# Two-layer diffusion backbone on one core: where the convolution filters and the Fourier part are computed

## Chip, cores and metric

One core of a Trainium2 chip runs the whole program in one launch. The metric is the device time of one execution in microseconds, median over runs. In the profile PE is TensorE, PEld its weight loads, DVE VectorE, ACT ScalarE, POOL GpSimd, SP SyncE.

## The reference

384 tokens (128 context, 256 latent) of width 1024 pass through two layers. A layer is a half-step feed-forward (SwiGLU, inner width 2816), a token mixer and another half-step feed-forward, each behind an RMS norm scaled and shifted by a modulation made from `c` (latent) or `c_ctx` (context). The mixer's heads are three groups: a Hyena convolution over 256 channels, neighbourhood attention (6 heads) and windowed grouped-query attention (6 query heads, 2 key heads). The convolution's filter depends on weights alone, not on x:

```python
hid  = sin(freq[0] * (feats @ w1 + b1))            # feats: L x 33
hid  = sin(freq[1] * (hid @ w2 + b2))              # L x 64
taps = (hid @ w3).reshape(L, 2, 256) * exp(-t * deltas)
kf   = rfft(concat(taps[:, 0], 0, taps[:0:-1, 1]))
x0, x1, v = split(short_conv(u)); z = x1 * v
y    = x0 * (irfft(rfft(z, 2L) * kf)[:L] + z * skip)   # context (L=128), latent (L=256)
```

## The kernel before

Activations lie with channels on partitions, 384 tokens in the free dimension; weights are float32, each split into a high and a low part, and `mm3` (L303) makes a product of three matmuls (L305 to L307). The weights' order is fixed in `jobs`; `issue`, `ahead` and `get` (L164 to L192) load them ahead through SP's queue, which brings all loads in the order in which they are written, into four buffers, and split them on ScalarE (L142) and VectorE (L143). Each engine executes its instructions in the order in which the Python code writes them.

**Start.** `start(j)` (L1133) prepares the eight chunks of the first feed-forward half; between two chunks' `up` products (18 matmuls each, 144 in all) it is called again, with `mid=True` inside them. The modulation of this half comes in three column chunks for scale and shift, q = 0 and 1: `chunk_load` (L262) loads them, `chunk_rows` (L272) multiplies them with `ct` on TensorE in groups of 32 columns (tile `adm`), `chunk_cols` (L283) turns rows to columns. `square_chunk` (L323), `stats1` and `stats2` make the reciprocal root of the mean square (`rsqrt`, L309; here on VectorE, elsewhere on GpSimd). Later modulation is made on VectorE (L206).

**Mixer.** `mixer(l)` (L536) writes seven projections (`project`, L708: four blocks of 2 k, or two of 4); after each block they call `work(budget)`. `bg` holds generators; `work` advances each one step, from the first on, as long as its budget, which each step's yielded cost lowers, is above nothing; `BUD` holds 1.55 and 3.3 for projections, 1.3 for attention.

```python
BUD = (1.55, 3.3, 1.3)
conv_it = add(conv_bg()); filt_it = add(filt())
drain(q_it); drain(k_it); drain(conv_it); drain(filt_it)
fft_it = add(fft())
```

`conv_bg` (L695) makes u and the short convolution, `filt` (L583) this layer's filter: two sine layers (`sin_layer`, L518), taps in three groups, spectrum (`tf`, 13 matmuls of 256 columns) into the tables K1, K2, K3. `na_post`, `gk_post` and `gq_post` norm and turn queries and keys. `drain` runs a generator to its end. Then `slot` (L972) is called 15 times: slot s writes the scores of unit s (12 units: six head pairs, two query blocks), the norm of unit s-1, the turn of the probabilities of s-2 (`un_turn`, L927: transposes into `pp`, copies into `PT`, which has two buffers), the values of s-3 when that pair is full (`un_pv`, L941), the exponentials, and `work(BUD[2])`. `fft` (L781) runs in these slots: turns of z, three transforms (`zf`) with six products on VectorE each (L809 to L814), two inverse transforms (`cv`, L821). Blocks of the output projection (`wout_block`, L1074) stand between the last slots; the one that needs the convolution's output comes behind `drain(fft_it)`.

Of the kernel before, what the change touches and what calls it, by code (L numbers as in the profile page):

```python
# [7 lines left out]
F32 = mybir.dt.float32  # L8
# [6 lines left out]
P = 128  # L15
# [32 lines left out]
HD = 64  # L48
# [11 lines left out]
for _name, _w in (  # L60
    ("ada_b", DEPTH * NADA * KD), ("norm_g", DEPTH * 3 * KD), ("conv_w", DEPTH * 3 * 6), ("conv_b", DEPTH * 6),
    ("skip", DEPTH * 2), ("naq", DEPTH), ("nak", DEPTH), ("fb1", DEPTH), ("fb2", DEPTH), ("freq", DEPTH * 2),
    ("fscale", 3), ("sel", 2),
):
    SM[_name] = (_n, _w)
    _n += _w
# [13 lines left out]
def _build(ctx, tc, nc, A):  # L80
# [6 lines left out]
    ptp = ctx.enter_context(tc.tile_pool(name="ptp", bufs=2))  # L87
# [29 lines left out]
    load(A["ct"], ct)  # L117
    for k in range(KD):
        load(A["xT"][:, k], xT[k])
    sml = cst.tile([P, NSM], F32, name="sml")  # L120
    load(A["sml"], sml)
    ident = cst.tile([P, P], F32, name="ident")
    load(A["ident"], ident)
# [13 lines left out]
    fw1 = cst.tile([33, DEPTH, HD], F32, name="fw1")  # L137
    fw2 = cst.tile([HD, DEPTH, HD], F32, name="fw2")
# [104 lines left out]
    S.activation(ct[:, :, 0:2], ct[:, :, 0:2], AF.Silu)  # L243
# [266 lines left out]
    fbm = []  # L510
    for l in range(DEPTH):
        fbm.append([cst.tile([P, 1], F32, name=f"fbm{l}{i}") for i in range(2)])

    def sin_bias(l):
        for i, nm in enumerate(("fb1", "fb2")):
            V.tensor_tensor(fbm[l][i], small(nm, l), small("freq", l * 2 + i), op=ALU.mult)

    def sin_layer(pin, fb, fr, out):  # L518
        arg = tt("arg", w=NT)[:HD]
        S.activation(arg, pin, AF.Identity, scale=fr[:HD], bias=fb[:HD])  # L520
        yield 0.1
        kq = tt("kq", w=NT)[:HD]
# [8 lines left out]
        yield 2.3  # L531
        S.activation(out, arg, AF.Sin)
        yield 0.1


    def mixer(l, after):  # L536
# [20 lines left out]
        def loads():  # L557
# [25 lines left out]
        def filt():  # L583
            Cc, Sc = (X["dft"][0][:, i * P:(i + 1) * P] for i in range(2))
            Cl, Sl = X["dft"][1:3], X["dft"][3:5]
# [789 lines left out]
```

## Time and profile before

| | us |
|---|---|
| median of three runs | 1543.93 |
| the runs | 1543.81, 1543.93, 1544.58 |
| the profiled execution | 1544.34 |
| its span, first to last instruction | 1542.6 |
| TensorE, VectorE, ScalarE, GpSimd busy | 1505.7, 1139.4, 672.6, 70.7 |

The busy times are sums over the span; where in it an engine waits, and for whom, has to be read from the timeline of that stretch. A matmul's time in it includes a tail that the next one overlaps, so that the distance from start to start is the better measure; x2 and the like are that many instructions in one row.

### The profile page before, as it was taken

The page shows a single profiled execution, that of the slowest core. Times are in us where ns is not written, and L with a number is a line of the kernel's source. Part 1 is how long each engine was busy: PE and PEld are TensorE (multiplying, and loading weights), DVE is VectorE, ACT ScalarE, POOL GpSimd, SP SyncE. Part 2 cuts the span into 40 slices and gives each one's busy share as a digit, 9 for nine tenths or more (in the row PEclk, how much of TensorE's full clock was granted, in tenths as well). Part 3 has the DMA queues.
Part 4 walks back from the last instruction along what each step waited for, and adds up shares of the span by engine and source line. Part 5 has one row for each costly group of instructions (what it writes and reads, how often), then busy time and mean ns, then how long its engine had stood idle before and what let it go on. Part 6 is the DMA issues. An engine that isn't in the chain of part 4 may idle for free. (4 is left out here: it accounts for less than half of the span.)

```text
span 1542.6 us, 23084 instructions
## 1 busy us (share of the span) xinstructions
PE 1505.7 (98%) x8652; PEld 1444.0 (94%) x8652; DVE 1139.4 (74%) x2158; ACT 672.6 (44%) x1234; POOL 70.7 (5%) x181
## 2 busy tenths in 40 slices
PE   6999999999989999999999999999999999999999
PEld 3999999999768999999999999999996699999998
DVE  4489888879787788877758898787897767544344
ACT  4533333446566454333434433343556655433221
POOL 0000000013300000000000000000141000000000
PEclk9999999999999999999999999999999999999999
DMA  9656665664403446555544565566543034343442
GB/s 307 236 184 237 219 223 201 218 195 149 129 30 117 153 148 220 207 212 187 187 162 139 188 244 209 207 221 202 172 124 109 26 111 138 134 149 108 149 152 72
DMA packets 89733, 261.27 MB, mean 169 GB/s; under 512 B 10097, under 2 KB 27796, under 8 KB 89492
## 3 DMA queue, kind: packets, MB, share of 16 engines
q1 hardware_dynamic: 89236, 258.74, 49.1%
q8 instruction: 68, 1.11, 0.3%
q0 software_dynamic: 384, 1.05, 0.2%
q14 instruction: 45, 0.37, 0.1%
HBM read 257.13 MB, written 2.62 MB: 168 GB/s over the span
## 5 line engine op out<-in xcount | busy, mean ns | idle before, releaser
L143 DVE TENSOR_TENSOR wlo<-raw,whi 128x1024 fp32r<-128x1024 f32 (+2 forms) x352 | 394.4, 1126 | 122.6 <-ACT whi L142 122.5
L305 PE MATMUL up<-mh,whi 128*128 128x384 f32 (+1 forms) x1408 | 479.3, 340 | 4.9 <-ACT mh L142 4.9
L306 PE MATMUL up<-ml,whi 128*128 128x384 f32 (+1 forms) x1408 | 477.4, 339 | 0.7 <-DVE ml L143 0.4
L307 PE MATMUL up<-mh,wlo 128*128 128x384 f32 (+1 forms) x1408 | 477.3, 339 | 0.8 <-DVE wlo L143 0.6
L142 ACT ACTIVATE whi<-raw 128x1024 fp32r<-128x1024 f32 (+2 forms) x352 | 338.4, 974 | 264.4 <-PE dn L306 128.2
L206 DVE CUSTOM_DVE_ANT_0 junk<-adaw,cb,sml 128x1024 bf16<-128x1024 f32 x256 | 332.7, 1300 | 1.9
L305 PEld LDWEIGHTS up<-mh,whi 128*128 128x128 f32 x1408 | 265.8, 189 | 8.7 <-ACT mh L142 6.3
L306 PEld LDWEIGHTS up<-ml,whi 128*128 128x128 f32 x1408 | 265.6, 189 | 2.5 <-DVE ml L143 2.1
L307 PEld LDWEIGHTS up<-mh,wlo 128*128 128x128 f32 x1408 | 266.0, 189 | 2.1 <-DVE wlo L143 2.1
L305 PE MATMUL dn<-gh,whi 128*128 128x384 f32 x704 | 237.4, 337 | 0.0
L306 PE MATMUL dn<-gl,whi 128*128 128x384 f32 x704 | 237.2, 337 | 0.0
L307 PE MATMUL dn<-gh,wlo 128*128 128x384 f32 x704 | 237.1, 337 | 0.0
L142 ACT ACTIVATE gh<-t 128x384 fp32r<-128x384 f32 x76 | 39.9, 525 | 273.0 <-DVE t L485 263.3
L307 PEld LDWEIGHTS dn<-gh,wlo 128*128 128x128 f32 x704 | 132.2, 188 | 0.0
L305 PEld LDWEIGHTS dn<-gh,whi 128*128 128x128 f32 x704 | 132.2, 188 | 0.0
L306 PEld LDWEIGHTS dn<-gl,whi 128*128 128x128 f32 x704 | 132.2, 188 | 0.0
L305 PE MATMUL pj<-whi,mh 128*128 128x384 f32 (+1 forms) x240 | 80.1, 334 | 1.0 <-DVE hyt L362 1.0
L485 DVE TENSOR_TENSOR t<-up,t 128x384 f32<-128x384 f32 x72 | 40.0, 556 | 55.0 <-PE up L307 54.8
L307 PE MATMUL pj<-whi,ml 128*128 128x384 f32 (+1 forms) x240 | 78.3, 326 | 0.0
L306 PE MATMUL pj<-wlo,mh 128*128 128x384 f32 (+1 forms) x240 | 78.2, 326 | 0.0
L143 DVE TENSOR_TENSOR gl<-t,gh 128x384 fp32r<-128x384 f32 x76 | 42.5, 559 | 45.0 <-ACT gh L142 45.0
L326 ACT ACTIVATE sq<-xT 128x384 f32<-128x384 f32 x42 | 22.0, 525 | 100.6 <-DVE xT L385 99.3
(222 smaller groups left out, 1582.9 us busy)
## 6 DMA issues: line engine op xcount, KB each, us to landing
raw<-w SPq DMA_DIRECT2D x184, 512.0 KB, 4.4
adaw<-ada SPq DMA_DIRECT2D x128, 512.0 KB, 3.5
raw<-w SPq DMA_DIRECT2D x64, 448.0 KB, 4.3
raw<-win SPq DMA_DIRECT2D x48, 384.0 KB, 4.0
raw<-w13a SPq DMA_DIRECT2D x32, 384.0 KB, 4.0
adw<-ada SPq DMA_DIRECT2D x32, 192.0 KB, 4.3
raw<-woa SPq DMA_DIRECT2D x16, 384.0 KB, 3.2
nab<-nab SPq DMA_DIRECT2D x24, 192.0 KB, 2.5
```

Source lines behind the costliest of these rows:

```text
L142: S.activation(hi, src, AF.Copy)
L143: V.tensor_tensor(lo, src, hi.bitcast(F32), op=ALU.subtract)
L206: V.tensor_tensor_reduce(out=junk, in0=w, in1=cb[:, v, :], scale=scale, scalar=small("ada_b", (l * NADA + p) * KD + j), op0=ALU.mult, op1= ...
L305: T.matmul(out, ah, bh, start=start, stop=False)
L306: T.matmul(out, ah, bl, start=False, stop=False)
L307: T.matmul(out, al, bh, start=False, stop=stop)
L326: S.activation(sq, xT[j], AF.Square)
L485: V.tensor_tensor(t1, PQ[1][:, :NT], t1, op=ALU.mult)
```

## The change

The new class `Filters` makes the filters of both layers in `start(0)`: the layers lie side by side (on 64 partitions each in the sine layers, on 256 columns each in the spectrum, so that a spectrum matmul has 512 columns), and the spectrum stays in `kft[0]` (in the buffer that later holds `PT`) and `kft[1]`. Both matrices of the third filter layer are loaded and their sum and difference `wsd` taken ahead of the product; the taps of token 0, which have one side only, are made by extra one-row operations. Its loads, sine layers, taps and spectrum are written ahead of the first `up` product, between the parts that were there. `filt`, its loads in the mixer and K3 are gone; `fft` mends row 0 for the first two transforms instead. `chunk_rows` takes scale and shift in one PSUM tile, `chunk_cols` both at once; the reciprocal root of the start goes to GpSimd (`stats1()`). `conv_bg` and `fft` are one generator, `hyena`, drained ahead of attention; in a slot the values of s-3 are written ahead of the turn of s-2, and `PT` has one buffer. The diff, without the host's tables and a few renamed tiles:

```diff
-    ptp = ctx.enter_context(tc.tile_pool(name="ptp", bufs=2))
+    ptp = ctx.enter_context(tc.tile_pool(name="ptp", bufs=1))
...
     def chunk_load(c):
         a, b = CHUNK[c]
         n = (b - a) * P
-        for q in range(2):
-            firsts[c, q] = [tt("adw", w=NT) for _ in range(KD)]
-            for k, t in enumerate(firsts[c, q]):
-                load(A["ada0"][q, k, :, a * P:b * P], t[:, :n])
+        firsts[c] = [[tt("adw", w=NT) for _ in range(2)] for _ in range(KD)]
+        for k in range(KD):
+            for q in range(2):
+                load(A["ada0"][q, k, :, a * P:b * P], firsts[c][k][q][:, :n])
 
     adm = {}
 
-    def chunk_rows(c, q):
+    def chunk_rows(c):
         a, b = CHUNK[c]
         n = (b - a) * P
-        pm = ps("adm", "ab"[q])
-        for k, t in enumerate(firsts.pop((c, q))):
-            o = 32 * (k % 4)
-            T.matmul(pm[o:o + 32, :n], ct[:, k], t[:, :n], start=(k < 4), stop=(k >= 4))
+        pm = ps("adm", "a")
+        for k, w in enumerate(firsts.pop(c)):
+            for q in range(2):
+                o = 64 * q + 32 * (k % 2)
+                T.matmul(pm[o:o + 32, :n], ct[:, k], w[q][:, :n], start=(k < 2), stop=(k >= KD - 2))
         rows = tt("adr", w=NT)
         S.activation(rows[:, :n], pm[:, :n], AF.Copy)
-        adm[c, q] = pm, rows
-
-    def chunk_cols(c, q):
+        adm[c] = pm, rows
+
+    def chunk_cols(c):
         a, b = CHUNK[c]
         n = b - a
-        pm, rows = adm.pop((c, q))
-        o = pm[:, NT:NT + 2 * n]
+        pm, rows = adm.pop(c)
+        o = pm[:, NT:NT + 4 * n]
         for i in range(n):
-            T.matmul(o[:, 2 * i:2 * i + 2], rows[:, i * P:(i + 1) * P], small("sel", 0, 2), start=True, stop=True)
-        o = o.rearrange("p (j v) -> p j v", v=2)
+            T.matmul(o[:, 4 * i:4 * i + 4], rows[:, i * P:(i + 1) * P], small("sel", 0, 4), start=True, stop=True)
+        o = o.rearrange("p (j q v) -> p j q v", q=2, v=2)
 
         def wide(t):
             return t.rearrange("p (j o) -> p j o", o=1).to_broadcast([P, n, 2])
 
-        if q:
-            V.tensor_tensor(mod[0][:, 0, a:b], o, wide(small("ada_b", a, n)), op=ALU.add)
-        else:
-            t = gsc[0][:, 0, a:b]
-            V.tensor_tensor(t, o, wide(small("norm_g", a, n)), op=ALU.mult)
-            V.tensor_tensor(t, t, wide(gb0[:, a:b]), op=ALU.add)
-        done.update((0, 1 - q, j) for j in range(a, b))
+        t = gsc[0][:, 0, a:b]
+        V.tensor_tensor(t, o[:, :, 0], wide(small("norm_g", a, n)), op=ALU.mult)
+        V.tensor_tensor(t, t, wide(gb0[:, a:b]), op=ALU.add)
+        V.tensor_tensor(mod[0][:, 0, a:b], o[:, :, 1], wide(small("ada_b", a, n)), op=ALU.add)
+        done.update((0, p, j) for p in range(2) for j in range(a, b))
 
...
-    def sin_layer(pin, fb, fr, out):
-        arg = tt("arg", w=NT)[:HD]
-        S.activation(arg, pin, AF.Identity, scale=fr[:HD], bias=fb[:HD])
-        yield 0.1
-        kq = tt("kq", w=NT)[:HD]
+    def sin_layer(pin, i, out):
+        fb = sm("fbm", 1)
+        V.tensor_tensor(fb, small("fb", i), small("freq", i), op=ALU.mult)
+        arg = tt("arg", w=NT)
+        S.activation(arg, pin, AF.Identity, scale=small("freq", i), bias=fb)
+        kq = tt("kq", w=NT)
...
+    class Filters:
+        def load_a(self):
+            self.fw1 = load(A["fw1"], tt("fw1", w=P)[:33])
+            self.feats = load(A["feats"], tt("feats", w=NT)[:33])
+            load(A["sml"], sml)
+            self.fw2 = load(A["fw2"], tt("fw2", w=HD))
+
+        def load_b(self):
+            self.w3 = [load(A["fw3"][:, i * HY:(i + 1) * HY], tt("w3", w=HY)) for i in range(2)]
+
+        def load_c(self):
+            decay = rawp.tile([P, 1024], F32, tag="raw", name="decay")
+            load(A["decay"], decay[:, :3 * HY].rearrange("p (t c) -> p t c", t=3))
+            self.decay = [decay[:, t * HY:(t + 1) * HY] for t in range(3)]
+            dftl = rawp.tile([P, 1024], F32, tag="raw", name="dftl")
+            load(A["dft1"][:, 0:4], dftl.rearrange("p (i c) -> p i c", i=4))
+            self.dftl = dftl
+            self.dft0 = load(A["dft0"][:, 0:2 * P], tt("dft0", w=2 * P))
+
+        def first(self):
+            p1 = ps("f1")
+            T.matmul(p1[:, :NT], self.fw1, self.feats, start=True, stop=True)
+            self.h1 = tt("h1", w=NT)
+            sin_layer(p1[:, :NT], 0, self.h1)
+
+        def second(self):
+            p2 = ps("f2")
+            for l in range(DEPTH):
+                r = slice(l * HD, (l + 1) * HD)
+                T.matmul(p2[r, :NT], self.fw2[r], self.h1[r], start=True, stop=True)
+            self.h2 = tt("h2", w=NT)
+            self.p2 = p2
+
+        def second_sin(self):
+            sin_layer(self.p2[:, :NT], 1, self.h2)
+            self.wsd = [tt("wsd", w=HY) for _ in range(2)]
+            V.tensor_tensor(self.wsd[0], self.w3[0], self.w3[1], op=ALU.add)
+            V.tensor_tensor(self.wsd[1], self.w3[1], self.w3[0], op=ALU.subtract)
+
+        def taps(self, t):
+            if t == 0:
+                self.sd = []
+            S2 = adap.tile([P, D], F32, tag="ada", name="taps")
+            S2 = S2.rearrange("p (i l c) -> p i l c", i=2, l=DEPTH)
+            self.sd.append(S2)
+            pt = [ps("taps") for _ in range(DEPTH)]
+            rows = [slice(l * HD, (l + 1) * HD) for l in range(DEPTH)]
+            c = slice(t * P, (t + 1) * P)
+            for i in range(2):
+                for l in range(DEPTH):
+                    T.matmul(
+                        pt[l][:, i * HY:(i + 1) * HY], self.h2[rows[l], c], self.wsd[i][rows[l]], start=True, stop=True
+                    )
+            dec = self.decay[t].rearrange("p (o c) -> p o c", o=1)
+            for l in range(DEPTH):
+                V.tensor_tensor(
+                    S2[:, :, l], pt[l].rearrange("p (i c) -> p i c", i=2), dec.to_broadcast([P, 2, HY]), op=ALU.mult
+                )
+            if t < 2:
+                p0 = [ps("tap0") for _ in range(DEPTH)]
+                for l in range(DEPTH):
+                    T.matmul(p0[l][0:1, :HY], self.h2[rows[l], t * P:t * P + 1], self.w3[0][rows[l]], start=True, stop=True)
+                for l in range(DEPTH):
+                    V.tensor_tensor(S2[0:1, 0, l], p0[l][0:1, :HY], self.decay[t][0:1], op=ALU.mult)
+                    V.scalar_tensor_tensor(
+                        S2[0:1, 1, l], p0[l][0:1, :HY], -1.0, self.decay[t][0:1], op0=ALU.mult, op1=ALU.mult
+                    )
+
+        def spectrum(self, ft):
+            if ft == 0:
+                kft[0] = ptp.tile([P, 1792], F32, tag="PT", name="kft0")[:, :6 * HY].rearrange("p (i c) -> p i c", i=6)
+            f = 0 if ft == 0 else ft - 1
+            fs = slice(f * P, (f + 1) * P)
+            if ft == 0:
+                C, Sn = [[(self.dft0[:, i * P:(i + 1) * P], 0)] for i in range(2)]
+            else:
+                C, Sn = [
+                    [(self.dftl[:, (2 * i + t) * HY:(2 * i + t + 1) * HY], 1 + t) for t in range(2)] for i in range(2)
+                ]
+            sc = small("fscale", ft)
+            for mats, which, row in ((C, 0, False), (Sn, 1, False), (Sn, 0, True)):
+                if row and ft == 2:
+                    continue
+                p = ps("kf")
+                o = p[0:1] if row else p
+                for n, (mat, t) in enumerate(mats):
+                    T.matmul(
+                        o, mat[:, 0:1] if row else mat[:, fs],
+                        self.sd[t][:, which].rearrange("p l c -> p (l c)"),
+                        start=(n == 0), stop=(n == len(mats) - 1),
+                    )
+                for l in range(DEPTH):
+                    d = kft[l][:, (0 if which == 0 and not row else 3) + ft]
+                    S.activation(
+                        d[0:1] if row else d, o[:, l * HY:(l + 1) * HY], AF.Copy, scale=sc[0:1] if row else sc
+                    )
+
+    filters = Filters()
 
...
-            X["feats"] = side(A["feats"], tt("feats", w=NT)[:33])
-            X["w3"] = [side(A["fw3"][:, l, i * HY:(i + 1) * HY], tt("w3", w=NT)[:HD, :HY]) for i in range(2)]
-            X["decay"] = [side(A["decay"][:, t], tt("decay", w=HY)) for t in range(3)]
...
-        def filt():
...
-            K1, K2, K3 = X["K"]
+            K1, K2 = kft[l][:, 0:3], kft[l][:, 3:6]
...
-                V.tensor_tensor(a, zr, K1[ft], op=ALU.mult)
-                V.tensor_tensor(b, zi, K2[ft], op=ALU.mult)
+                V.tensor_tensor(a, zr, K1[:, ft], op=ALU.mult)
+                V.tensor_tensor(b, zi, K2[:, ft], op=ALU.mult)
+                V.tensor_tensor(c, zi, K1[:, ft], op=ALU.mult)
+                V.tensor_tensor(d, zr, K2[:, ft], op=ALU.mult)
+                if ft < 2:
+                    V.tensor_tensor(c[0:1], zi[0:1], K2[0:1, ft], op=ALU.mult)
+                    V.memset(b[0:1], 0.0)
+                    V.memset(d[0:1], 0.0)
                 V.tensor_tensor(a, a, b, op=ALU.add)
-                V.tensor_tensor(c, zi, K3[ft], op=ALU.mult)
-                V.tensor_tensor(d, zr, K2[ft], op=ALU.mult)
                 V.tensor_tensor(c, c, d, op=ALU.subtract)
...
-        conv_it = add(conv_bg())
-        filt_it = add(filt())
+        def hyena():
+            yield from conv_bg()
+            yield 0.05
+            yield from fft()
+
+        hy_it = add(hyena())
...
+            if 0 <= s - 3 < len(hs) and hs[s - 3].qi:
+                un_pv(hs[s - 3])
             if 0 <= s - 2 < len(hs):
                 un_turn(hs[s - 2])
-            if 0 <= s - 3 < len(hs) and hs[s - 3].qi:
-                un_pv(hs[s - 3])
...
-        drain(conv_it)
-        drain(filt_it)
-        fft_it = add(fft())
+        drain(hy_it)
 
...
-        drain(fft_it)
...
     def start(j, mid=False):
         if mid:
-            if j in (2, 5):
-                c = (j + 1) // 3
-                chunk_cols(c, 1)
-                for k in range(*CHUNK[c]):
-                    start_h(k)
-        elif j == 0:
+            if j in (1, 4):
+                chunk_rows((j + 2) // 3)
+            return
+        if j == 0:
+            F = filters
+            F.load_a()
+            for c in range(KD // 2):
+                load(A["xT"][:, c], xT[c])
+            F.load_b()
+            for c in range(KD // 2, KD):
+                load(A["xT"][:, c], xT[c])
+            F.load_c()
+            load(A["ident"], ident)
+            load(A["ct"], ct)
             chunk_load(0)
+            issue(2)
+            F.first()
+            for c in range(3):
+                square_chunk(c)
+            F.second()
+            F.second_sin()
+            for c in range(3, KD):
+                square_chunk(c)
+            S.activation(ct[:, :, 0:2], ct[:, :, 0:2], AF.Silu)
+            r = stats1()
+            for t in range(3):
+                F.taps(t)
+            ada_tables(0)
+            chunk_load(1)
+            F.spectrum(0)
+            R = stats2(r)
+            start_x(0, R)
+            ahead(1)
+            F.spectrum(1)
+            start_x(1, R)
+            chunk_rows(0)
+            F.spectrum(2)
+            chunk_cols(0)
+            start_h(0)
+            start_h(1)
+            ahead(2)
             issue(3)
-            chunk_load(1)
-            for c in range(KD):
-                square_chunk(c)
-            ada_tables(0)
-            chunk_rows(0, 0)
-            r = stats1(V)
-            chunk_cols(0, 0)
-            chunk_rows(0, 1)
-            R = stats2(r)
-            chunk_cols(0, 1)
-            ahead(1)
-            for c in range(3):
+            chunk_load(2)
+            for c in range(2, KD):
                 start_x(c, R)
-                start_h(c)
-            ahead(2)
-            issue(4)
-            chunk_load(2)
-            for c in range(3, KD):
-                start_x(c, R)
-        elif j in (1, 4):
-            chunk_rows((j + 2) // 3, 0)
-        elif j in (2, 5):
-            chunk_cols((j + 1) // 3, 0)
-            chunk_rows((j + 1) // 3, 1)
-        elif j == 6:
-            load(A["fw1"], fw1)
-            load(A["fw2"], fw2)
+            return
+        if j in (2, 5):
+            chunk_cols((j + 1) // 3)
+        if j + 1 < KD:
+            start_h(j + 1)
+        if j == 6:
             load(A["crow"], cb)
```

## Rows read from the trace of the kernel before

**Rows 1.** The page's head and its section 1: span, busy time of each engine.

```profile
span 1542.6 us, 23084 instructions
...
PE 1505.7 (98%) x8652; PEld 1444.0 (94%) x8652; DVE 1139.4 (74%) x2158; ACT 672.6 (44%) x1234; POOL 70.7 (5%) x181
```

**Rows 2.** Table by stretch: stretch, length, busy PE, PEld, DVE, ACT, POOL, clock, DMA, GB/s.

```profile
400.00:450.00 50.00, 46.05 (x263) 34.19 (x262) 39.52 (x130) 31.09 (x87) 6.14 (x16) 0.93 0.29 86
600.00:700.00 100.00, 100.00 (x573) 100.00 (x572) 81.20 (x120) 35.77 (x50) 0.00 (x0) 1.00 0.60 217
```

**Rows 3.** Timeline, start: start, length, engine, line, operation, out<-in, count, [idle before].

```profile
6.55 2.61 ACT L326 ACTIVATE sq<-xT 128x384 f32<-128x384 f32 x5 [0.20 <-DMA xT<-xT]
...
16.82 2.97 PE L278 MATMUL adm<-adw,cb 128*32 128x384 f32 x16
...
25.38 0.69 PE L305 MATMUL up<-mh,whi 128*128 128x384 f32 x1 [3.78 <-ACT mh L142]
...
29.66 0.50 PE L305 MATMUL up<-mh,whi 128*128 128x384 f32 x1
...
29.98 0.36 PE L306 MATMUL up<-ml,whi 128*128 128x384 f32 x1
...
30.71 0.34 PE L307 MATMUL up<-mh,wlo 128*128 128x384 f32 x1
...
30.98 1.50 PE L278 MATMUL adm<-adw,cb 128*32 128x384 f32 x16
```

**Rows 4.** Timeline: the 144th and the 145th matmul of the first feed-forward half.

```profile
62.18 0.34 PE L307 MATMUL up<-mh,wlo 128*128 128x384 f32 x1
...
62.35 0.34 PE L305 MATMUL up<-mh,whi 128*128 128x384 f32 x1
```

**Rows 5.** Timeline: the filter of layer 0 in the projections, its first layers and taps.

```profile
345.84 0.85 PE L590 MATMUL f<-feats,fw 33*64 33x384 f32 x2
...
351.36 0.34 DVE L523 TENSOR_SCALAR kq<-arg 64x384 f32<-64x384 f32 x1
...
354.27 0.53 ACT L532 ACTIVATE h<-arg 64x384 f32<-64x384 f32 x1 [3.34 <-DVE arg L530]
...
379.33 1.13 PE L601 MATMUL taps<-w,h 64*128 64x256 f32 x4
```

**Rows 6.** Timeline of TensorE: two pairs of spectrum matmuls in the projections.

```profile
402.90 0.59 PE L621 MATMUL kf<-ts,dft 128*128 128x256 f32 x2
403.33 0.59 PE L621 MATMUL kf<-td,dft 128*128 128x256 f32 x2
```

**Rows 7.** Timeline of TensorE: attention of layer 0.

```profile
415.76 0.92 PE L885 MATMUL sc<-kTN,qTN 64*128 64x384 f32 x4
...
428.67 1.24 PE L885 MATMUL sc<-kTN,qTN 64*128 64x384 f32 x4
...
439.44 0.92 PE L885 MATMUL sc<-kTG,qTG 64*128 64x384 f32 x4
...
446.07 0.39 PE L821 MATMUL cv<-dft,ya 128*128 128x128 f32 x2
...
451.46 0.92 PE L885 MATMUL sc<-kTG,qTG 64*128 64x384 f32 x4
...
460.21 0.97 PE L885 MATMUL sc<-kTG,qTG 64*128 64x384 f32 x3 [0.84 <-ACT PT L939]
...
471.06 0.55 PE L934 MATMUL pp<-ident,pr 128*128 128x128 f32 x3
```

**Rows 8.** Timeline of VectorE: first and last of a transform's six products.

```profile
429.44 0.42 DVE L809 TENSOR_TENSOR ya<-zf,K 128x256 f32<-128x256 f32 x1
...
431.35 0.42 DVE L814 TENSOR_TENSOR yc<-yc,yd 128x256 f32<-128x256 f32 x1
```

**Rows 9.** Timeline of GpSimd: first and last of a reciprocal root's thirteen steps.

```profile
519.42 0.75 POOL L315 TENSOR_SCALAR rs_r<-rs_r 128x3 int32<-128x3 int32 x1 [106.03 <-DVE rs_r L314]
...
524.02 0.20 POOL L320 TENSOR_TENSOR rs_r<-rs_r,rs_t 128x3 f32<-128x3 f32 x1
```

More of the change, by code (lines that the diff above doesn't have):

```diff
@@ L116, in _build @@
     ct = cb[:, 0, :KD * 32].rearrange("p (k o) -> p k o", o=32)
-    load(A["ct"], ct)
-    for k in range(KD):
-        load(A["xT"][:, k], xT[k])
     sml = cst.tile([P, NSM], F32, name="sml")
-    load(A["sml"], sml)
     ident = cst.tile([P, P], F32, name="ident")
-    load(A["ident"], ident)
+    kft = [None, cst.tile([P, 6, HY], F32, name="kft1")]
     def small(name, i, n=1):
@@ L581, in loads3 @@
             X["vcG"] = side(A["kvG"][l, :, P:], tt("vcG", w=P))
-        def filt():
-            Cc, Sc = (X["dft"][0][:, i * P:(i + 1) * P] for i in range(2))
-            Cl, Sl = X["dft"][1:3], X["dft"][3:5]
-            decay, w3 = X["decay"], X["w3"]
-            K1, K2, K3 = ([tt(f"K{i}", w=HY) for _ in range(n)] for i, n in ((1, 3), (2, 3), (3, 2)))
-            X["K"] = K1, K2, K3 + [K1[2]]
-            p1 = ps("f1")
-            T.matmul(p1[:HD, :NT], fw1[:, l], X["feats"], start=True, stop=True)
-            h1 = tt("h1", w=NT)
-            yield from sin_layer(p1[:HD, :NT], fbm[l][0], small("freq", l * 2), h1[:HD])
-            p2 = ps("f2")
-            T.matmul(p2[:HD, :NT], fw2[:, l], h1[:HD], start=True, stop=True)
-            h2 = tt("h2", w=NT)
-            yield from sin_layer(p2[:HD, :NT], fbm[l][1], small("freq", l * 2 + 1), h2[:HD])
-            sd = []
-            for t in range(3):
-                pt = ps("taps")
-                for i in range(2):
-                    T.matmul(
-                        pt[:, i * HY:(i + 1) * HY], h2[:HD, t * P:(t + 1) * P], w3[i][:HD, :HY], start=True, stop=True
-                    )
-                t0, t1 = tt("tp0", w=HY), tt("tp1", w=HY)
-                V.tensor_tensor(t0, pt[:, :HY], decay[t], op=ALU.mult)
-                V.tensor_tensor(t1, pt[:, HY:], decay[t], op=ALU.mult)
-                if t < 2:
-                    V.memset(t1[0:1], 0.0)
-                s, d = tt("ts", w=HY), tt("td", w=HY)
-                V.tensor_tensor(s, t0, t1, op=ALU.add)
-                V.tensor_tensor(d, t1, t0, op=ALU.subtract)
-                sd.append((s, d))
-                yield 1.4
-            yield 0.1
-            def tf(dst, ft, mats, which, row=False):
-                p = ps("kf")
-                o = p[0:1, :HY] if row else p[:, :HY]
-                sc = small("fscale", ft)
-                for n, (mat, t) in enumerate(mats):
-                    T.matmul(o, mat, sd[t][which], start=(n == 0), stop=(n == len(mats) - 1))
-                S.activation(dst[ft][0:1] if row else dst[ft], o, AF.Copy, scale=sc[0:1] if row else sc)
-            tf(K1, 0, [(Cc, 0)], 0)
-            tf(K2, 0, [(Sc, 0)], 1)
-            V.memset(K2[0][0:1], 0.0)
-            V.tensor_copy(K3[0], K1[0])
-            tf(K3, 0, [(Sc[:, 0:1], 0)], 0, True)
-            for i in range(2):
-                yield 0.2
-                c = slice(i * P, (i + 1) * P)
-                tf(K1, 1 + i, [(Cl[0][:, c], 1), (Cl[1][:, c], 2)], 0)
-                tf(K2, 1 + i, [(Sl[0][:, c], 1), (Sl[1][:, c], 2)], 1)
-                if i == 0:
-                    V.memset(K2[1][0:1], 0.0)
-                    V.tensor_copy(K3[1], K1[1])
-                    tf(K3, 1, [(Sl[0][:, 0:1], 1), (Sl[1][:, 0:1], 2)], 0, True)
-            yield 0.2
@@ L640, in mixer @@
         loads()
-        sin_bias(l)
         nq8 = sm("nq8", 1)
@@ L1291, in _layout @@
     put("nak", np.tile(np.asarray(I["na_k_g"]).T, (2, 1)))
[L1292 to L1294 removed]
+    put("fb", np.stack([np.asarray(I["hy_filt_b1"]).reshape(P), np.asarray(I["hy_filt_b2"]).reshape(P)], 1))
+    put("freq", np.asarray(I["hy_freq"]).transpose(0, 2, 1).reshape(P, 2))
     put("fscale", fscale)
[L1296 removed]
+    row, col = np.arange(P)[:, None], np.arange(4)[None]
+    put("sel", ((row // 64 == col // 2) & (row % 32 == col % 2)).astype(f32))
     a["sml"] = sml
```

22 lines of the change are left out of this document (3 added, 19 removed).

## The prediction

> **What bounds the kernel now.** I read the page first: TensorE is busy for 98% of 1542.6 us [rows 1]. That alone would say that every matmul taken away is time taken away. The table by stretch shows where it isn't so [rows 2]: in a feed-forward stretch TensorE is busy throughout at a granted clock of 1.00, with matmuls 0.17 us apart [rows 4], and the change touches nothing there; from 400 to 450 us (end of the projections, first half of attention) it is busy for 46.05 of 50, and VectorE for 39.52. So three places have to be read closely: the start up to the end of the first 144 matmuls, the projections of a mixer, and attention. The second layer's mixer runs the same code on the same shapes; I work out the first and double it.
>
> **The start.** Now the queue brings x and 3 MB of the first modulation chunk, the last of its matmuls ends at 16.82 + 2.97 = 19.8 us, the first real matmul comes at 25.38 and the 145th at 62.35 [rows 3, 4]. The change puts all filter work of both layers ahead of that first matmul, and TensorE executes in order: whatever is written before it has to be over.
> Loads: 1.41 MB more stand ahead of the chunk (constants, third filter matrix, decay). x comes at about 192 KB per 0.6 us (five squares, paced by it, took 2.61 [rows 3]), so the chunk is complete some 4.8 us later, at about 25. That turns out not to be last.
> Sine layers: feats and the small table, now first in the queue, land at about 4 us. One f matmul takes 0.85 with its tail [rows 5], and double at the half clock at which the rested engine starts (1.2 GHz, 0.32 us per matmul until 29.98 [rows 3]); with about 0.65 for the Identity and 3.44 us from the first of six VectorE steps to the end of Sin (351.36 to 354.80 [rows 5]) the first layer ends at 9.4. Three squares of 0.52 now stand ahead of the second Identity on ScalarE, two adds ahead of its chain on VectorE; it ends at 16.2. The five last squares are written behind the second Sin, so the sum of squares, now ready by 10, ends at 19.7, and its column sums at 21. The reciprocal root goes to GpSimd: 519.42 to 524.22, 4.8 us [rows 9], hence 26.6; nobody waits so long for it, as VectorE comes to the diagonal later:
> Taps: VectorE has six products of 128x512 (a 128x256 one is 0.42 [rows 8]; about 0.67 each) and eight one-row ones of about 0.36: 6.9 us, fed by TensorE with two waits of about 1 us for PSUM, from 22.6 to 29.5; then six small table steps (1.0) and the diagonal (0.66): 31.1.
> TensorE behind it: 0.65 for the row sums, six spectrum matmuls, the chunk's 16 matmuls, four more of the spectrum, the column turns. A spectrum matmul of 256 columns takes 0.43 (402.90 to 403.33 [rows 6]), so one of 512 columns 0.86. 31.2 + 0.65 + 5.2 + 2.7 + 3.4 + 0.8 = 44.0; three small VectorE steps 0.5 and three ScalarE ones 1.5: first matmul at **46.1**, 20.7 late. Of 13 spectrum matmuls only the first three lie beside other work.
> The block of 144 gains: it takes 37.0 us now; then 144 x 0.174 = 25.1, two chunks of 2.7 (8 matmuls took 1.50 [rows 3]), 1.2 of column turns and 0.3 of waits, 32.0. It gains 5.0, of which 2.3 because the clock is up by then. **Start: +15.7.** With every wait on the way gone (TensorE without a break from 21, 18.6 us of work, 2.0 behind) it is +11.2; 4 us later at the half clock, +20.
> Switching: a matmul of 32-column quarters starts 0.27 us behind a full one, where 0.17 is usual, at 30.71 and 30.98 [rows 3]. The Trainium skill, TensorEngine Tiling (Array Packing), Tiling Modes, says that a change of tiling mode drains TensorE, a change of tile alone doesn't. The new start has about a dozen such changes between 33-row, 64-row, full and 32-column forms; by 0.10 each they add 1.2 us, which I leave to the range.
>
> **The mixers, each.** Out of the projections: two f matmuls 1.6, three groups of taps 3.2 (1.13 each with a tail [rows 5]), 13 spectrum matmuls of 0.43 with their weight changes 6.0, in all 10.8 us, of which the last 1.8 stand behind the last projection matmul, ahead of the first score at 415.76 [rows 7]. TensorE waits little there, so the other 9.0 are time. The background generators advance one step for each call, and filter and convolution advanced side by side; convolution and Fourier part are now one generator. Counting steps, the turns of z come in the first block of the last projection, the three transforms in the next three, and the two inverse transforms (cv) are left to the drain ahead of attention. So into the projections go the turns 0.8, two waits of 0.6 for their copies (the projection holds three of the four banks of that tag), transforms of 0.86 and 1.72: 4.6. **Projections: -4.4.**
> Between last projection matmul and first score: now 1.8 us. Then the third transform 1.72, a wait of 2.5 for its six VectorE steps (429.44 to 431.77 [rows 8]), two cv of 2.2 (446.07 to about 448.2 [rows 7]): 8.6. **+6.8.** This wait is new, and all that TensorE has left stands behind it. The first minimum of the scores then waits on VectorE for the second cv's products, written ahead of it (four of about 0.4, a ScalarE copy and its remainder, 0.5 each): **+2.0**.
> Attention itself loses 10.7 us of TensorE work (turns 0.8, transforms 5.5, of which the first ran at the half clock, cv 4.4) and 11 us of VectorE work (three times 2.3, twice 2.1). Is that time? Pairs of slots start at 428.67, 439.44, 451.46, 460.21 and 471.06 [rows 7]. The last of these pairs, 10.85 us, has no Fourier work but an output-projection block of 3.4; a pair of its own takes 7.4, with TensorE idle 0.84 us for a copy at its head [rows 7]: it is the chain of score, minimum, exponential, norm, turn and copy. By that floor the pairs give back 1.4 (8.75), 1.2 (12.02 less 3.4) and 2.2 (10.77; its GQA turn comes later, since two GQA scaling steps slip from the projections into the slots); the four first slots, 12.9 us, lose 2.6 of TensorE work and give about 1.7. **-6.5**, between -3 (the turn's copies late behind the values' 1.7 us) and -10.7 (all of it). The single buffer costs nothing of its own: the values' matmuls are now written ahead of the turn that overwrites what they read.
> **A mixer: -4.4 + 6.8 + 2.0 - 6.5 = -2.1; both: -4.2** (from +3 to -17).
>
> **Sum.** 1544.34 us (the profiled execution: 1542.6 of span and 1.7 around it) + 15.7 - 4.2 = 1555.8; that execution is 0.4 over the median of the runs shown, hence **1555.4**.
>
> **The rivals.** (B) Attention is bound by TensorE, as the page's 98% suggests: it gives all 10.7, and the delayed minimum costs nothing; a mixer gives 4.4 - 6.8 + 10.7 = 8.3, both 16.6, and the time is 1543.0. Against it: the idle in a pair that holds no Fourier work. It turns to faster from 18.8 on.
> (C) Faster: the filters really are covered by the loading. Place: TensorE's queue ahead of the chunk's matmuls. If both spectrum groups were over when the chunk lands at 25, the first matmul would come at about 28, and with the block's 5.0 the start would be 2.4 shorter: 1537.3. It takes the chain of two sine layers, squares, taps and spectrum to end 18 us before my count; it decides for faster once the start costs under 1.1. For it: TensorE idles for much of the time until 25.38. Against: every link of the chain has its row.
> (D) Slower still: TensorE stays at 1.2 GHz in the filters as it did at 25.38 (part of 13 spectrum matmuls at 1.7 instead of 0.86: +4) and attention gives only 3 each (+7): 1566. For it: TensorE works in scraps until 27 us.
> That the Fourier part isn't ahead of attention in earnest is part of my count: its last two steps are, but uncovered.
>
> **How the numbers follow.** Chances: forecast 0.55, B 0.16, C 0.12, D 0.17. A difference of 0.2% (3.1 us) is about what can be told from none. Faster: C and 0.05 of B, 0.17. Same: the rest of B and 0.03 of the forecast's edge, 0.14. Slower: 0.69. The range, 1541 to 1566, takes in B and D up to its middle, and leaves out C and the far side of D.
>
> **What would show it.** Right: first `up` matmul at 44 to 48 us, with spectrum matmuls of 0.86 before it; the 145th near 78; TensorE idle 2 to 3 us ahead of the first cv, two cv in a row, then the scores; pairs of about 7.4 us in attention, more idle ahead of turns; mixers 1 to 4 us shorter each. Wrong: a first matmul before 40 us, or pairs that shrink by as much as the Fourier work in them. The least certain terms are the 6.5 and the waits in the taps.

## The result, and the profile after

The changed kernel takes 1556.88 us (median) against 1544.19 us for the kernel before: a ratio of 1.0082, 95% interval 1.0065 to 1.0100: slower by 0.8%. 1555.4 was forecast. In its profiled execution (1557.04 us) TensorE does 2.5 us less work in a span that is 12.7 us longer [rows 1]; head of the page after:

```profile
span 1555.3 us, 22995 instructions
...
PE 1503.2 (97%) x8616; PEld 1443.7 (93%) x8616; DVE 1131.0 (73%) x2123; ACT 671.9 (43%) x1229; POOL 73.1 (5%) x194
```

Timeline of TensorE from the start, kernel after (start, length, engine, line, operation, out<-in, count, idle before):

```profile
3.02 1.61 PE L538 MATMUL f<-feats,fw 33*128 33x384 f32 x2 [3.02 <-DMA feats<-feats]
9.41 1.55 PE L546 MATMUL f<-h,fw 64*64 64x384 f32 x4 [4.77 <-ACT h L515]
19.50 1.44 PE L332 MATMUL pss<-ones,accq 128*128 128x1 f32 x6 [8.54 <-DVE accq L319]
20.86 2.08 PE L567 MATMUL taps<-wsd,h 64*128 64x256 f32 x8
...
28.03 2.93 PE L603 MATMUL kf<-taps,dft 128*128 128x512 f32 x6
30.89 0.91 PE L344 MATMUL pr<-dg,ones 128*128 128x384 f32 x2
31.64 4.97 PE L603 MATMUL kf<-taps,dftl 128*128 128x512 f32 x11
36.03 0.85 PE L271 MATMUL adm<-adw,cb 128*32 128x384 f32 x6
...
39.55 3.70 PE L603 MATMUL kf<-taps,dftl 128*128 128x512 f32 x8
43.09 0.73 PE L282 MATMUL adm<-sml,adr 128*128 128x4 f32 x6
45.99 0.69 PE L296 MATMUL up<-mh,whi 128*128 128x384 f32 x1 [2.17 <-ACT mh L135]
...
47.39 0.52 PE L296 MATMUL up<-mh,whi 128*128 128x384 f32 x1
47.71 0.52 PE L297 MATMUL up<-ml,whi 128*128 128x384 f32 x1
...
80.41 0.34 PE L296 MATMUL up<-mh,whi 128*128 128x384 f32 x1
```

The first real matmul comes at 45.99 us where it came at 25.38 [rows 3], the 145th at 80.41 where it came at 62.35 [rows 4]. From 19.5 us on TensorE has no gap to speak of until 43.8; then it waits 2.17 us for the first prepared chunk, and the matmuls behind the wait stand 0.32 us apart, not 0.17. The table by stretch of the same kernel (stretch, length, busy PE, PEld, DVE, ACT, POOL, granted clock, DMA, GB/s) shows why: the granted clock is 0.50 there, TensorE's lower level of 1.2 GHz.

```profile
36.00:46.00 10.00, 7.83 (x50) 3.44 (x48) 0.43 (x4) 4.67 (x12) 0.00 (x0) 0.98 0.21 75
46.00:52.00 6.00, 6.00 (x18) 5.69 (x19) 4.95 (x10) 5.05 (x9) 0.00 (x0) 0.50 0.83 252
52.00:60.00 8.00, 8.00 (x64) 5.97 (x63) 3.47 (x7) 1.63 (x4) 0.00 (x0) 0.97 0.61 204
```

The mixer of layer 0, from the last projection matmul on, in the timeline of the kernel after:

```profile
426.58 0.33 PE L298 MATMUL pj<-whi,ml 128*128 128x384 f32 x1
...
426.75 1.89 PE L823 MATMUL zf<-zT,dft 128*128 128x256 f32 x8
428.48 0.38 PE L844 MATMUL cv<-dft,ya 128*128 128x128 f32 x2
...
430.48 0.70 PE L847 MATMUL cv<-dft,ya 128*128 128x256 f32 x2 [0.53 <-DVE ya L836]
...
433.71 0.92 PE L912 MATMUL sc<-kTN,qTN 64*128 64x384 f32 x4
...
436.82 0.55 DVE L923 CUSTOM_DVE_ANT_0 pr<-sc,nab 128x384 f32<-128x384 f32 x1
```

Third transform, both inverse transforms, then the scores (at 415.76 before [rows 7]), and VectorE's first minimum 3.1 us behind these. In the kernel before it came 1.2 us behind them (timeline of VectorE, before):

```profile
416.93 0.56 DVE L896 CUSTOM_DVE_ANT_0 pr<-sc,nab 128x384 f32<-128x384 f32 x1 [2.71 <-PE sc L888]
```

Further on, two rows of the timelines of TensorE and VectorE, kernel after, show a wait that the prediction's sum hardly has:

```profile
458.08 0.47 PE L772 MATMUL gt<-ident,ra 128*128 128x128 f32 x1 [4.51 <-DVE ra L1034]
```

```profile
461.88 0.56 DVE L923 CUSTOM_DVE_ANT_0 pr<-sc,gmask 128x384 f32<-128x384 f32 x1 [3.85 <-PE sc L915]
```

TensorE waits 4.51 us for the last rotated queries of grouped attention; then VectorE waits 3.85 us for the scores that stood behind them. Over this wait the clock falls once more (table by stretch, kernel after):

```profile
455.00:462.00 7.00, 3.92 (x17) 2.77 (x19) 3.08 (x12) 2.50 (x7) 0.00 (x0) 0.52 0.00 0
```

Stretches in us, from the starts of the matmuls that bound them in each trace; layer 0 / layer 1. The projections are counted from the first matmul of a tile `pj`, behind the one for u, which takes 27 us in every kernel; the whole mixer goes from there to the next `up`:

| kernel | 145th `up` | projections | last of them to first score | first score to last values | whole mixer |
|---|---|---|---|---|---|
| before | 62.35 | 72.29 / 71.89 | 1.99 / 2.00 | 60.95 / 59.43 | 162.90 / 161.07 |
| after | 80.41 | 66.88 / 66.38 | 7.13 / 7.14 | 58.05 / 57.38 | 159.89 / 158.56 |
| `fft_in_slots` | 80.27 | 62.25 / 61.76 | 0.27 / 0.27 | 62.38 / 61.40 | 152.66 / 151.13 |
| `gq_ahead` | 79.45 | 64.83 / 64.29 | 10.28 / 10.28 | 52.01 / 51.40 | 154.93 / 153.73 |

18.06 at the start, less 3.01 and 2.51 in the mixers: 12.5 of the 12.7 us. The feed-forward stretches between differ by at most 0.5 us.

### The profile page after: what moved, and what is told of

It is laid out like the page before. It is cut to its first block, busy times and chain, and to the rows that moved or that the text cites. A ratio compares the mean times of both kernels' runs of the same rounds, so it can differ in the third digit from the quotient of the medians.

```text
span 1555.3 us, 22995 instructions
## 1 busy us (share of the span) xinstructions
PE 1503.2 (97%) x8616; PEld 1443.7 (93%) x8616; DVE 1131.0 (73%) x2123; ACT 671.9 (43%) x1229; POOL 73.1 (5%) x194
## 4 chain that ended last, share of the span: by engine, by line
PE 82%; DVE 10%; ACT 5%; issue 2%; DMA 1%; SPq 0%; POOL 0%; DVEq 0%; ACTq 0%; POOLq 0%
PE up L298 14%; PE up L296 14%; PE up L297 14%; PE dn L296 8%; PE dn L297 8%; PE dn L298 8%; PE pj L296 3%; PE pj L298 2%; PE pj L297 2%; DVE wlo L136 2%; ACT whi L135 1%; DVE junk L199 1%; DVE ml L136 1%; DVE pr L900 1%; DVE pr L923 1%
## 5 line engine op out<-in xcount | busy, mean ns | idle before, releaser
L306 POOL TENSOR_SCALAR rs_r<-rs_r 128x3 int32<-128x3 int32 (+2 forms) x14 | 8.5, 607 | 1194.0 <-DVE rs_r L305 738.9
```

Source lines behind the costliest of these rows:

```text
L306: G.tensor_scalar(r.bitcast(I32), r.bitcast(I32), -1.0, float(0x5F3759DF), op0=ALU.mult, op1=ALU.add)
```

## The experiments

All are the changed kernel, or the run that is named, with the edit shown; medians are of their own runs, beside 1544.4 to 1544.7 us for the kernel before.

**The start: what the gap costs.** `fill_gap`

```diff
-            F.spectrum(2)
             chunk_cols(0)
             start_h(0)
             start_h(1)
+            F.spectrum(2)
```

> The changed kernel with the third spectrum group written behind the modulation's column turns and the first two prepared chunks instead of ahead of them. My theory (TensorE's 2.17 us without work at 43.8 us is what sends it to 1.2 GHz, at which the first 20 matmuls run, 0.32 us each): the spectrum matmuls cover that wait, the first up matmul comes at about 44.7 instead of 46.0 and runs at 0.17 us, the 145th at about 76.4 instead of 80.4; 1552.9 us. Rival (the clock falls because of the work ahead, not of the gap): the first up matmul is 1.3 us earlier and the 20 still take 0.32 us each; 1555.6 us.

1554.06 us. Timeline of TensorE and the table by stretch, kernel `fill_gap`:

```profile
41.39 3.68 PE L603 MATMUL kf<-taps,dftl 128*128 128x512 f32 x8
44.51 0.74 PE L296 MATMUL up<-mh,whi 128*128 128x384 f32 x1
45.08 0.33 PE L297 MATMUL up<-ml,whi 128*128 128x384 f32 x1
45.25 0.34 PE L298 MATMUL up<-mh,wlo 128*128 128x384 f32 x1
```

```profile
44.00:52.00 8.00, 8.00 (x58) 5.83 (x60) 5.50 (x11) 6.23 (x13) 0.00 (x0) 1.00 0.68 201
```

No wait, clock 1.00, 0.17 us from matmul to matmul; the 145th is 3.50 us earlier (76.91), 1.48 of it the gap and 2.02 the rate. The gap was what sent TensorE down to 1.2 GHz. The Trainium skill, TensorE: Matmul & The Clock Gate, Why this matters for your kernels, advises leaving no idle gaps between bursts of matmuls lest they run at half rate. The gaps it warns of are longer than this one; the measurement decides, 0.50 behind the gap of 2.17 us and 1.00 without it.

**The start: the chain ahead.** `taps_first`

```diff
+            F.taps(0)
             r = stats1()
-            for t in range(3):
+            for t in range(1, 3):
                 F.taps(t)
```

> The changed kernel with the first group of taps written ahead of the column sums of x's squares instead of behind them. My theory (from 19.5 us on TensorE works without a break up to 43.8 and VectorE's products hang on the taps, so that everything that starts earlier brings the first up matmul forward): taps begin at 16 us, VectorE's first product comes at 19.5 instead of 23.0, right behind its sum of squares, the first up matmul at about 42.6, 1553.5 us. Rival (something else is due at that time, the modulation chunk's load or the diagonal behind the reciprocal root): the first up matmul stays at 46, 1556.9 us.

1555.18 us. Timeline of TensorE, and one row of VectorE's, kernel `taps_first`:

```profile
15.90 2.08 PE L567 MATMUL taps<-wsd,h 64*128 64x256 f32 x8 [4.90 <-ACT h L515]
...
42.55 0.44 PE L296 MATMUL up<-mh,whi 128*128 128x384 f32 x1 [2.17 <-ACT mh L135]
```

```profile
19.42 1.28 DVE L572 TENSOR_TENSOR taps<-taps,decay 128x512 f32<-128x512 f32 x2
```

VectorE's product comes at 19.42 (22.97 in the kernel after), the first `up` at 42.55, as expected: the filter's chain set the start, not a load. The 145th is 4.50 us earlier, the end of the program only 2.2 in its trace: 1.2 us of attention in layer 0 and 1.1 of the feed-forward stretch between the layers are longer here. That stretch is 591.6 to 593.1 us over the traces of all these kernels, which run the same code there, so I take the loss for scatter between executions; that isn't shown.

**The start: filter work or loads.** `no_filters`, and `no_filters_no_loads` with the last two lines (the loads) out as well; the tables `kft` are set to zero on GpSimd.

```diff
-            F.first()
...
-            F.second()
-            F.second_sin()
...
-            for t in range(3):
-                F.taps(t)
...
-            F.spectrum(0)
...
-            F.spectrum(1)
...
-            F.spectrum(2)
...
-            F.load_b()
...
-            F.load_c()
```

> The changed kernel with the filter work of both layers left out (sine layers, taps and spectrum aren't computed, the filter tables are set to zero); its loads, the merged modulation rows and the reciprocal root on GpSimd stay. My theory (the 18.1 us that the 145th matmul came later are filter work on TensorE and on the chain ahead of it, not loads): the first chunk lands at about 25 us, the first up matmul comes at about 28.5, the 145th at about 62.5, 1539 us. Rival (a good part of the 18 us is the 1.41 MB of loads written ahead of the first modulation chunk, or the root on GpSimd): the 145th at 68 us or later, 1545 us or more.

> The kernel without filter work (tables set to zero), and without the loads of the third filter matrix, decay and transform matrices at the start (1.28 MB) as well. It asks what the 5.4 us are by which the 145th matmul came later than before although no filter work was left. Theory L (the first modulation chunk lands later behind these loads): they go nearly whole, first up matmul at about 26, 145th at about 63. Theory G (the reciprocal root on GpSimd, 3.5 us, and behind it in TensorE's order the 32 matmuls of the modulation rows at the half clock, 5.2 us): the first up matmul stays at 29 to 30, the 145th at 65 or later.

Timelines of TensorE, `no_filters` and then `no_filters_no_loads`:

```profile
18.81 1.65 PE L344 MATMUL pr<-dg,ones 128*128 128x384 f32 x2 [4.77 <-DMA adw<-ada]
20.39 5.21 PE L271 MATMUL adm<-adw,cb 128*32 128x384 f32 x32
26.99 0.83 PE L282 MATMUL adm<-sml,adr 128*128 128x4 f32 x6 [1.40 <-ACT adr L273]
30.00 0.45 PE L296 MATMUL up<-mh,whi 128*128 128x384 f32 x1 [2.17 <-ACT mh L135]
...
50.84 0.68 PE L296 MATMUL up<-mh,whi 128*128 128x384 f32 x1 [2.50 <-ACT mh L135]
```

```profile
19.57 4.31 PE L271 MATMUL adm<-adw,cb 128*32 128x384 f32 x32
24.58 0.83 PE L282 MATMUL adm<-sml,adr 128*128 128x4 f32 x6 [0.70 <-ACT adr L273]
27.59 0.69 PE L296 MATMUL up<-mh,whi 128*128 128x384 f32 x1 [2.17 <-ACT mh L135]
```

The 145th comes at 67.71 and 65.30. So of the 18.06 us 12.70 are filter work (80.41 - 67.71), 2.41 loads, and 2.95 neither. The 12.70 are net: the first `up` alone moves by 15.99 (45.99 - 30.00), but without filters the block of 144 takes 37.71 us instead of 34.42, mainly since TensorE waits 2.50 us more at 50.84 for a prepared chunk. My expectation of 62.5 was 5.2 us off and the rival is right about "a good part", though not in full; without the loads too, the result (27.59 and 65.30) lies between the two theories. In the last 2.95 may lie the rows' matmuls behind the diagonal in TensorE's order, the reciprocal root on GpSimd, merged rows and a second wait as at 50.84; these weren't taken apart. `no_filters` takes 1545.34 us (1540.34 without the loads too): the mixers' gain just pays for the start that is left.

**The mixer: Fourier part back in the slots.** `fft_in_slots`

```diff
-NTP = 50
+NTP = 46
...
-    kft = [None, cst.tile([P, 6, HY], F32, name="kft1")]
+    kft = [cst.tile([P, 6, HY], F32, name=f"kft{i}") for i in range(DEPTH)]
...
-            yield from fft()
...
         drain(hy_it)
+        fft_it = add(fft())
...
+        drain(fft_it)
         wout_block(po, 3, 2, 2)
```

> The changed kernel with the Fourier part back in the slots of attention, as a generator of its own, as before; both filter tables in buffers of their own, and 46 instead of 50 general buffers to make room. My theory (attention is bound by the chain of score, minimum, exponential, norm, turn and copy, and by VectorE; Fourier work in it is nearly free): per mixer the projections lose about 4.6 us more, the stretch from the last projection matmul to the first score falls from 7.1 to about 1, and first score to last value matmul, 58.1 us in layer 0 now, goes back to about 61; together -8.2 per mixer, 1540.5 us. Rival (attention is bound by TensorE, so Fourier work costs there what it costs elsewhere): first score to last value matmul about 68.8 us, time about 1556, no gain.

1541.86 us, ratio to the kernel before 0.9982 (0.9973 to 0.9991). The projections lose 4.63 us, the stretch behind them 6.86, and attention takes back 4.33: my numbers, not the rival's. By this alone attention seems to hold the Fourier part at 40% of its TensorE time. The next run says otherwise.

**The mixer: the new wait.** `gq_ahead`

```diff
-        gq_it = add(gq_post(pg))
+        gq_it = add(gq_post(pg), True)
```

> The changed kernel with the grouped queries' norm and rotation put ahead of convolution and Fourier part in the background order. My theory (the 4.51 us that TensorE waits ahead of the seventh slot are the price of the Fourier part's place in that order: the rotation was pushed out of the projections into the slots and is due there): the wait goes to under 1 us, Fourier steps slip into the drain ahead of attention, where the 7.1 us become 9 to 10; net -1 to -2 per mixer, 1553 to 1555 us. Rival (VectorE has that work to do in any case and is what bounds the first slots): the wait goes, but the slots ahead of it aren't shorter, 1557 us or more.

1547.22 us, 9.7 less. The stretch to the first score grew by 3.15 us and the projections fell by 2.05, as expected in kind; attention fell by 6.0 in both layers, and there I was wrong by a factor. Here two scalings (2.3 us of VectorE's) are back ahead of the scores, and no rotation is left to the drain: the rotated queries' turn waits 0.49 us where it waited 4.51, and VectorE's 3.85 us without work are gone as well. So is the second fall of the clock: 1.00 from there on. Timeline of TensorE and a row of the table by stretch, `gq_ahead`:

```profile
451.38 0.33 PE L772 MATMUL gt<-ident,pj 128*128 128x128 f32 x1 [0.49 <-ACT pr L940]
```

```profile
445.80:485.90 40.10, 37.44 (x265) 26.01 (x263) 34.98 (x122) 30.43 (x94) 0.00 (x0) 1.00 0.07 24
```

`gq_ahead` and `fft_in_slots` have the same steps of grouped attention in the same slots, so they differ there by the Fourier part, and by about 1.9 us of VectorE's other work (one scaling, one split of weights) that in `fft_in_slots` runs behind the first score. Tables by stretch from first score to last values, `fft_in_slots` and `gq_ahead`:

```profile
421.94:484.30 62.36, 54.48 (x347) 39.18 (x347) 56.13 (x189) 40.26 (x119) 0.40 (x1) 0.95 0.17 54
```

```profile
433.86:485.90 52.04, 46.18 (x298) 31.68 (x297) 45.90 (x158) 37.86 (x115) 0.00 (x0) 0.93 0.15 49
```

10.3 us of time for 8.3 us of TensorE's work and 10.2 of VectorE's: the Fourier part was not nearly free in attention, it cost about what it takes of either engine. My theory falls.

**Which engine?** `fft_in_slots` without the products (first edit) and without the forward transforms (second edit):

```diff
-                V.tensor_tensor(a, zr, K1[:, ft], op=ALU.mult)
...
-                Yf.append((a, c))
+                Yf.append((zT[0], zT[1]))
```

```diff
-                pre = ps("zf", spare[0] if TAGS[1] else "b")
...
-                zr, zi = pre[:, :HY], pre[:, HY:]
+                zr, zi = zT[ft], zT[(ft + 1) % 3]
```

> The kernel with the Fourier part in attention's slots, without VectorE's products of spectrum and filter (24 a mixer; the inverse transforms read the turned z instead); all of TensorE's transforms stay. It asks why first score to last value matmul takes 62.4 us with the Fourier part in the slots and 52.0 without it and with the same grouped-query work there (10.4 for 10.2 us of VectorE work and 8.3 of TensorE work less). Theory V (VectorE's order bounds attention): about 8 us of products go, the stretch falls to 54 or 55 us. Theory T (TensorE does): it stays within 2 us of 62.4.

> The same kernel, with all of VectorE's products and without the three forward transforms on TensorE (10 matmuls of 256 columns a mixer, 0.43 us each; the products read the turned z instead). Theory V: first score to last value matmul stays at 61 to 62.4 us. Theory T: it falls by what they take, 4.3 us, to 58.

First score to last values: 59.27 us without the products and 61.10 without the transforms (layer 1: 58.02 and 59.98); the whole programs take 1535.96 and 1540.33 us. 8 us of VectorE's work bring 3.1, 4.3 of TensorE's 1.3: both theories missed the first run, and the second fits the one that has VectorE as the limit. That doesn't settle which engine it is, because the clock moved along. Tables by stretch from first score to last values, `slots_no_products` and `slots_no_transforms`:

```profile
421.30:480.57 59.27, 51.87 (x348) 37.53 (x347) 48.83 (x165) 39.71 (x119) 0.42 (x1) 1.00 0.18 57
```

```profile
421.93:483.03 61.10, 54.00 (x328) 37.05 (x327) 56.06 (x189) 40.47 (x119) 0.39 (x1) 0.89 0.17 57
```

The granted clock is 0.95 in `fft_in_slots`, 1.00 without the products and 0.89 without the transforms. So TensorE, with all its matmuls left, is busy for 2.6 us less without the products, and without 4.3 us of its own work for only 0.5 less. In these three stretches and in that of `gq_ahead` the time is TensorE's busy time and 5.9 to 7.9 us more, which speaks for TensorE, its clock included, rather than for VectorE. Why the clock differed isn't shown, and no run holds it still; nor was the part of ScalarE tried. What the inverse transforms and the gating behind them cost, the remaining 6 of 10.4 if the parts add, wasn't measured alone.

`best_gqa_early` (on top of `best`) tests VectorE's side in another way:

```diff
-        vN = project(384, 2, whole)
+        vN = project(384, 2, lambda kb: (whole(kb), whole(kb)))
```

> The fastest kernel so far with the background advanced twice instead of once behind each block of the last projection, so that the grouped queries' third scaling and both rotations (4.6 us of VectorE work a mixer) are made in the projections and not in the first slots of attention. Theory V: VectorE has room in the projections (54 of 66 us) and none in attention: first score to last value matmul falls by 3 to 4.6 us in each mixer, 1529 to 1532 us. Theory T: TensorE's work is the same, so nothing or half a microsecond, 1537 to 1538 us.

1539.72 us, where `best` (below) takes 1537.99; the intervals of their ratios to the kernel before overlap a little (0.9960 to 0.9980, 0.9939 to 0.9964), so it isn't faster, and that it is slower is only likely. First score to last values takes 63.86 us in its trace instead of 62.39. The background had got a step too far: the turn of the rotated queries now stands in the first slot, and TensorE waits there for rotations still queued on VectorE. Timeline of TensorE, `best_gqa_early`:

```profile
420.75 0.33 PE L770 MATMUL gt<-ident,ra 128*128 128x128 f32 x1 [1.47 <-DVE ra L1031]
424.27 0.48 PE L770 MATMUL gt<-ident,ra 128*128 128x128 f32 x1 [3.20 <-DVE ra L1031]
```

One row of its VectorE timeline says why they couldn't be earlier: in the last block of the projections VectorE waits for the queries' reciprocal root on GpSimd.

```profile
416.01 0.56 DVE L762 TENSOR_TENSOR pj<-pj,rs_r 128x384 f32<-128x384 f32 x1 [3.77 <-POOL rs_r L311]
```

**Buffer and order.** `turn_first` (45 general buffers)

```diff
-    ptp = ctx.enter_context(tc.tile_pool(name="ptp", bufs=1))
+    ptp = ctx.enter_context(tc.tile_pool(name="ptp", bufs=2))
...
+            if 0 <= s - 2 < len(hs):
+                un_turn(hs[s - 2])
             if 0 <= s - 3 < len(hs) and hs[s - 3].qi:
                 un_pv(hs[s - 3])
-            if 0 <= s - 2 < len(hs):
-                un_turn(hs[s - 2])
```

> The changed kernel with the turn of the probabilities written ahead of the values again, and two buffers of turned probabilities as before (45 general buffers to make room). My theory (buffer and order change nothing of their own: nobody waits for the buffer, and the values' 1.7 us ahead of a turn lie where the turn waits for its norm anyway): 1556.9 us within 1.5. Rival (the copies of the turn come late behind the values, up to 1.7 us in each of five pairs of both mixers): faster by 5 us or more.

1556.18 us, attention 57.73 and 56.49 us: within 0.9 us of the kernel after in each layer. No more than that hangs on the two together; they weren't tried apart.

**Together.** `best` is `fft_in_slots`, `fill_gap` and `taps_first` in one.

> The three edits that gained, together: Fourier part in the slots of attention (46 general buffers), third spectrum group behind the prepared chunks, first taps ahead of the column sums. My theory (the edits lie in different places, and the two of the start add: first up matmul at about 41.1 us at 0.17 us per matmul, 145th at about 72.5): 1541.9 - 2.8 - 1.7 to -3.4, so 1535.7 to 1537.4 us, faster than the kernel before by 0.5%. Rival (what the start gains is given back in the feed-forward halves, as two thirds of the 4.5 us of the taps edit were by the end): the 145th matmul as said, but 1540 us or more.

1537.99 us, ratio to the kernel before 0.9952 (0.9939 to 0.9964), the fastest kernel here that does all the work. First `up` at 41.86 and the 145th at 74.39, 0.8 and 1.9 us later than expected. The spectrum starts at 25.54 here and at 24.59 in `taps_first`, because TensorE is at the lower clock there, though what is written up to there is the same but for buffers; why isn't shown. Tables by stretch, `best` and `taps_first`:

```profile
22.50:26.00 3.50, 3.50 (x14) 2.06 (x14) 2.89 (x7) 0.00 (x0) 2.40 (x13) 0.51 0.94 337
```

```profile
22.50:26.00 3.50, 3.50 (x17) 1.70 (x16) 3.50 (x10) 0.25 (x1) 2.40 (x13) 1.00 1.01 344
```

The other 1.1 us I had counted twice: of the 4.50 us of `taps_first`, 1.06 were a shorter block (33.36 us instead of 34.42, fewer matmuls at the lower clock), and `fill_gap` (block 32.40) takes the same loss away; here the block takes 32.53. The mixers are those of `fft_in_slots` within 0.4 us.

## Why the prediction was right

**Start.** The chain was right link by link: first sine layer to 9.35 (9.4 forecast), second to 15.8 (16.2), products from 22.97 to 29.4 (22.6 to 29.5), first `up` at 45.99 (46.1). No term for changes of tiling mode was in that sum, and it came out 0.1 us over; that sets no price on them, since other links may hold it. The step that failed is the one behind it: "of which 2.3 because the clock is up by then". It wasn't; the prediction had counted the 2 us without work ahead of the first matmul and not asked what they do to the clock. The block took 34.4 us instead of 32.0, so +18.1 instead of +15.7; with the gap filled it takes 32.4.

**Projections and the stretch behind them.** Forecast -4.4 and +6.8, measured -5.4 and +5.1: in sum 2.7 us better. Removing the filter was worth 11.8 (72.29 - 62.25 and 1.99 - 0.27, by `fft_in_slots`; 10.8 forecast), Fourier work into the projections 4.63 (4.6 forecast), and the drain 6.86 (8.6 forecast): the wait of 2.5 us for VectorE was only 0.53, since the inverse transform's matmuls on the first two spectra run meanwhile.

**Attention.** -4.5 forecast (-6.5 for the work, +2.0 for the delayed minimum, which did come 1.9 us later behind the scores), -2.9 and -2.1 measured. This near hit is two errors that cancel. The work was worth far more than 6.5: without it, and with the queries in time, attention is 8.9 and 8.0 us shorter than before with the delay already in, so rival B, with 10.7, had the better of that step. The floor of 7.4 us for a pair, on which mine stood, came from one pair [rows 7]; in the kernel after, a pair without a block takes 6.26 (scores at 470.11 and 476.37). What held the change back is a wait that I named and priced at 1.2 us ("its GQA turn comes later": 2.2 for that pair, where 10.77 less the floor of 7.4 is 3.4): with it gone, and the clock behind it up, attention is 6.0 us shorter a mixer. The total is near by luck as well: against the forecast +2.4 us at the start, -5.4 in both layers' projections and the stretches behind them, +4.0 in attention.

**Rivals.** C didn't happen: the chain took until 43.8 us. D's half clock came, after the gap and not in the spectrum, where eight instructions take 0.44 us each with the gaps (3.54 us from 39.55 to 43.09). B's total (1543.0) failed mainly by that one wait and the start.

## What to carry to other kernels

Work put into a background queue displaces what stood there: list what slips, to which instruction it is due, and which in-order engine waits at that point; here that cost 6 us of a 9 us gain. A short wait of TensorE's can cost twice, once itself and once in clock, and independent work written into it was worth more than its length here. Taking a load off a pipeline in which two engines alternate is to be costed from a run without the load, and such runs are compared with the granted clock of the stretch beside them: here it moved between 0.89 and 1.00 with the edit.

## What the runs showed of the hardware

A wait of 2.17 us was enough for the matmuls behind it to run at 1.2 GHz (0.32 us instead of 0.17) for some 6 us, after almost unbroken work from 28.0 to 43.8 us, the last of it at a granted clock of 0.98. In `taps_first` the same 2.17 us brought about ten such matmuls, in the kernel after about twenty. In attention the granted clock fell to 0.52 over the 4.51 us wait, and stayed at 1.00 in the same place where that wait was 0.49 us.
